# When the first token pair chooses its experts and when the first experts load, in a two-layer hybrid block

## The chip, the cores and the metric

The kernel runs on one core of one Trainium2 chip. The metric is the device time of one execution in microseconds (us); lower is better. Several executions are timed and their median is quoted; one further execution is recorded by the hardware profiler, and all rows below come from that one.

## The reference

Two layers act on 512 tokens of width 1024, in float32. Each layer mixes the tokens in three ways (block-sparse attention, a gated delta rule, a convolution), joins the three results to 1024 columns and multiplies them by `w_out`, the output projection. Then a hierarchical mixture of experts follows: each token picks one of 4 groups and the best 2 of the group's 8 experts.

```python
mix = jnp.concatenate([y_nsa, y_gdn, y_conf], axis=-1) @ w_out[l]
x = _layer_norm(DEEPNORM_ALPHA * x + mix, ln1_w[l], ln1_b[l])
moe = _hier_moe(x, ...)      # softmax over 4 groups, top 1; top 2 of 8 experts; gated FFN of width 512
x = _layer_norm(DEEPNORM_ALPHA * x + moe, ln2_w[l], ln2_b[l])
```

## The kernel before, in words

The tokens lie in four tiles of 128. The output projection (lines 1109 to 1162) works on them in two **pairs**, `pr` 0 and 1. For each pair it goes through `w_out` in four slices of 256 rows (`i`, 1 MB each), and each slice holds two blocks of 128 rows. So a pair has eight blocks. For a block, ScalarE casts the weights to a rounded high part (`wo_hi`, line 1135), VectorE or GpSimd subtracts that from the weights to get the rest (`wo_lo`, line 1136; GpSimd for rows `k` 1, 4 and 7), and TensorE does twelve matmuls (`mm3`, lines 355 to 357: three per token tile and half of the columns, into `opA` and `opB`). A matmul that reads `wo_lo` is line 356.

Three buffers bound how far ahead the weights can be prepared. The slices lie in a ring of three 1 MB tiles (`ring`, line 160), so a slice is loaded only when the third slice before it has been cast and subtracted. The tiles `wo_hi` and `wo_lo` share a ring of six (`WL`), so a block is cast only when TensorE is done with the third block before it. And the load instruction itself waits in SyncE's queue, which is in order.

After a pair's matmuls, lines 1142 to 1161 add the residual, transpose the two tiles, multiply them by the router's weights (`r_ps`, line 1155), normalize, and store the normalized tiles to `x1D` in HBM through SyncE's queue (line 1158). They leave the router's logits of the pair in `lg`. Then `top_k` (lines 1081 to 1107) chooses the experts of these two tiles: some 30 small VectorE instructions on 128 by 2 to 128 by 128 elements, with two exponentials on ScalarE in between (lines 1096 and 1098). It writes the selection `selb` and the weights `sw`. Both are used only after the second pair, from line 1203 on, where the tokens are counted per expert and ranked.

`load_expert` (lines 1180 to 1195) loads one expert: four tiles of gate and up weights (line 1187, two DMAs of 512 KB each) and two of down weights (line 1192, 1 MB each), six tiles of 1 MB. Two experts have fixed numbers (`N_STATIC`) and are loaded at line 1197; the other loads need numbers that are computed from the choice. Their tiles rotate through `ring` (3, the tiles that `w_out` used), `ring2` (9, free since the attention ended) and `ring3` (1). So of the twelve tiles of the first two experts three need the last three slices of `w_out` to be done, and nine do not. The buffers into which tokens are gathered are cleared on GpSimd (line 1201); they take the place of two tiles that hold parts of the mixed tokens, so a clear waits for the last matmul that reads those.

The order of each engine's instructions is not written by hand here. A scheduler goes through the program, with a forecast of its own for every duration, and gives each engine the instruction that is ready first by that forecast, and among ready ones the one that stands earlier in the program. Every engine and every DMA queue then runs its list in order. Only from the first expert on is TensorE's order that of the program (line 1511).

```python
for pr in range(2):                            # lines 1111 to 1162, shortened
    for i in range(4):
        nc.sync.dma_start(w, w_out[l, ...])    # 1126
        for kk in range(2):
            A.copy(hi[:, :1024], src)          # 1135
            (G if k in (1, 4, 7) else V).tensor_tensor(lo[:, :1024], src, hi, op=ALU.subtract)
            mm3(...)                           # 1139
    lg = osm("r_lg", [P, 2, 36])
    ...
    top_k(lg, 2 * pr)                          # 1162
weights = {30 + e: load_expert(e) for e in range(N_STATIC)}    # 1197
```

Of the kernel before, what the change touches and what calls it, by code (L numbers as in the profile page):

```python
# [29 lines left out]
N_STATIC = 2  # L30
# [82 lines left out]
def hybrid_kernel(ctx, tc, x_in, w_in, w_out, cmp_pe, cmp_w1, cmp_w2, conv_w, a_log, dt_bias, norm_w,  # L113
                  dw_w, dw_b, cln_w, cln_b, ln1_w, ln1_b, ln2_w, ln2_b, w_grp, b_grp, w_exp, b_exp,
                  w_gate, w_up, w_down, consts, out, R=3, R2=9, R4=1, NG=10, NE=9, WL=6, layers=DEPTH, CN=32, GI=2, CV0=5, CV1=30, CVM="A", EB=12, SC="GAGA", LB2="GGVVVVVV", TO="0123", HL=3, LOP=4, LOM="10110101", XP=6, ORDER="GkGcomGqPwfx0yG1t2z3GGr"):
    nc = tc.nc
# [25 lines left out]
    def tp(key, tag, bufs, name=None, dt=F32, n=1024):  # L142
        return pl[key].tile([P, n], dt, tag=tag, name=name or tag, bufs=bufs)
# [7 lines left out]
    def x4(name):  # L151
        return xp.tile([P, 1056], F32, tag="x4", name=name)
# [7 lines left out]
    def wring(name):  # L160
        return ring.tile([P, 2048], F32, tag="w", name=name)
# [10 lines left out]
    def bank2(name):  # L172
        return pl["psA"].tile([P, 2, 512], F32, tag="a", name=name)
# [16 lines left out]
    def C(name):  # L190
        o, n = _OFF[name]
        return cst[:, o - P:o - P + n] if o < _RES else cst2[:, o - _RES - S:o - _RES - S + n]
# [32 lines left out]
    def bc(ap, n):  # L225
        return ap.unsqueeze(len(ap.shape)).to_broadcast(list(ap.shape) + [n])
# [78 lines left out]
    for l in range(layers):  # L305
# [5 lines left out]
        for kp in range(4):  # L311
            a = tp("inp", "xT", 8, f"xTh{kp}", F32R)
            b = tp("inp", "xT", 8, f"xTl{kp}", F32R)
            for kk in range(2):
                k = 2 * kp + kk
# [494 lines left out]
        for step in ORDER:  # L810
# [175 lines left out]
            elif step in '0123':  # L986
# [14 lines left out]
                for g in range(2):  # L1001
# [3 lines left out]
                    for b in range(2):  # L1005
# [6 lines left out]
                        for i0 in range(0, 4, hb):  # L1012
                            ps = bankS("a_s")
                            for i in range(hb):
                                o = i * P if t == 0 else i * 256
                                w = min(Lc, 512 - o)
# [8 lines left out]
                            for i in range(hb):  # L1025
                                e = tp("att", "e", EB, n=512)
# [39 lines left out]
        def osm(name, shape, dt=F32, bufs=2):  # L1066
            return pl["osm"].tile(shape, dt, tag=name, name=name, bufs=bufs)
# [5 lines left out]
        def first_max(src, rev, mx, oh, scr):  # L1073
            V.tensor_reduce(mx, src, axis=AX.X, op=ALU.max)
            for t in range(2):
                V.scalar_tensor_tensor(scr[:, t, :], src[:, t, :], mx[:, t:t + 1], rev, op0=ALU.is_equal, op1=ALU.mult)
            mv = osm("r_mv", [P, 2])
            V.tensor_reduce(mv, scr, axis=AX.X, op=ALU.max)
            V.tensor_tensor(oh, scr, bc(mv, src.shape[2]), op=ALU.is_equal)

        def top_k(lg, t0):
            zg, ze = lg[:, :, 0:4], lg[:, :, 4:36]
            s4, ohg = osm("r_s4", [P, 2, 4]), osm("r_ohg", [P, 2, 4])
            mg, gw, m1, m2 = [osm(n, [P, 2]) for n in ("r_mg", "r_gw", "r_m1", "r_m2")]
            em, s32, oh1, oh2 = [osm(n, [P, 2, 32]) for n in ("r_em", "r_s32", "r_oh1", "r_oh2")]
            first_max(zg, C("rev4"), mg, ohg, s4)
            V.tensor_scalar(ohg, ohg, 1.0, -NEG, op0=ALU.subtract, op1=ALU.mult)
            V.tensor_tensor(em.rearrange("p t (g e) -> p t g e", e=8), ze.rearrange("p t (g e) -> p t g e", e=8), bc(ohg, 8),
                            op=ALU.add)
            first_max(em, C("rev32"), m1, oh1, s32)  # L1090
            V.scalar_tensor_tensor(em, oh1, 2.0 * NEG, em, op0=ALU.mult, op1=ALU.add)
            first_max(em, C("rev32"), m2, oh2, s32)
            V.tensor_tensor(selb[:, t0:t0 + 2], oh1.unsqueeze(2).to_broadcast([P, 2, 2, 32]),
                            oh2.unsqueeze(2).to_broadcast([P, 2, 2, 32]), op=ALU.add)
            V.tensor_tensor(s4, zg, bc(mg, 4), op=ALU.subtract)
            A.activation(s4, s4, AF.Exp)
            V.tensor_tensor(m2, m2, m1, op=ALU.subtract)
            A.activation(m2, m2, AF.Exp)
            V.tensor_reduce(gw, s4, axis=AX.X, op=ALU.add)
            V.reciprocal(gw, gw)  # L1100
            V.tensor_scalar(m1, m2, 1.0, None, op0=ALU.add)
            V.reciprocal(m1, m1)
            V.tensor_tensor(m1, m1, gw, op=ALU.mult)
            V.tensor_tensor(m2, m2, m1, op=ALU.mult)
            V.tensor_tensor(oh1, oh1, bc(m1, 32), op=ALU.mult)
            V.tensor_tensor(oh2, oh2, bc(m2, 32), op=ALU.mult)
            V.tensor_tensor(sw[:, t0:t0 + 2, 1, :], oh1, oh2, op=ALU.add)
# [3 lines left out]
        for pr in range(2):  # L1111
            for t in (2 * pr, 2 * pr + 1):
                xt = x4(f"xr{t}")
                A.dma_start(xt[:, :D], xsrc[t * P:(t + 1) * P, :])
                xr.append(xt)
            def lt(i, k, t):
                if k < 4:
                    return mp[t // 2][i][:, (t % 2) * 512 + k * P:(t % 2) * 512 + (k + 1) * P]
                return mp["GC"[(k - 4) // 2]][i][:, (k % 2) * 512 + t * P:(k % 2) * 512 + (t + 1) * P]

            ap = [bank2("opA"), bank2("opB")]
            for i in range(4):

                kq = (3, 0, 1, 2)[i]
                w = wring("w_out")
                nc.sync.dma_start(w.rearrange("p (k c) -> p k c", k=2),
                                  w_out[l, kq * 256:(kq + 1) * 256, :].rearrange("(k p) c -> p k c", p=P))
                if pr == 0 and i == 1:
                    for n, src in ((1, mxA[1]), ("G", mxG)):
                        mp[n] = mix_parts(src, tp("out", "mh", 2, dt=F32R)[:, :D], "mxA")  # L1130
                for kk in range(2):
                    k = 2 * kq + kk
                    src = w[:, kk * 1024:(kk + 1) * 1024]
                    hi, lo = tp("out", "whl", WL, "wo_hi", F32R), tp("out", "whl", WL, "wo_lo", F32R)
                    A.copy(hi[:, :1024], src)
                    (G if k in (1, 4, 7) else V).tensor_tensor(lo[:, :1024], src, hi[:, :1024].bitcast(F32), op=ALU.subtract)
                    for t in (2 * pr, 2 * pr + 1):
                        for n in range(2):
                            mm3(ap[t % 2][:, n, :], lt(0, k, t), lt(1, k, t), hi[:, n * 512:(n + 1) * 512],
                                lo[:, n * 512:(n + 1) * 512], i == 0 and kk == 0, i == 3 and kk == 1)  # L1140

            lg = osm("r_lg", [P, 2, 36])
            for t in (2 * pr, 2 * pr + 1):
                V.scalar_tensor_tensor(xr[t][:, :D], xr[t][:, :D], ALPHA, ap[t % 2].rearrange("p a b -> p (a b)"),
                                       op0=ALU.mult, op1=ALU.add)
            for t in (2 * pr, 2 * pr + 1):
                xT = tp("osm", "x1T", 2)
                for kq in range(2):
                    ps = bank("x1T_ps")
                    for kk in range(4):  # L1150
                        T.transpose(ps[:, kk * P:(kk + 1) * P], xr[t][:, 4 * kq + kk:1024:8], ident)
                    A.copy(xT[:, kq * 512:(kq + 1) * 512], ps)
                ps = bank("r_ps")
                for k in range(8):
                    T.matmul(ps[:, 0:36], xT[:, k * P:(k + 1) * P], wrw[:, k, :], start=(k == 0), stop=(k == 7))
                mu, rs, nb = norm_stats([xr[t][:, h * 512:(h + 1) * 512] for h in range(2)])
                A.activation(xr[t][:, :D], xr[t][:, :D], AF.Identity, scale=rs, bias=nb)
                nc.sync.dma_start(x1D[l][t * P:(t + 1) * P, :], xr[t][:, :D])
                d = osm("r_d", [P, 36])
                V.scalar_tensor_tensor(d, cs, mu, ps[:, 0:36], op0=ALU.mult, op1=ALU.add)  # L1160
                V.scalar_tensor_tensor(lg[:, t % 2, :], d, rs, rb2, op0=ALU.mult, op1=ALU.add)
            top_k(lg, 2 * pr)
        outR.close()
        outL.close()
        mixer.close()
# [14 lines left out]
        def load_expert(e):  # L1180

            wgu, wd = [], []
            s_ = slice(e, e + 1) if isinstance(e, int) else bass.ds(e, 1)
            for i in range(4):
                w = ering("w_gu")
                for wi, src in enumerate((w_gate, w_up)):
                    nc.sync.dma_start(w[:, wi * 1024:(wi + 1) * 1024].rearrange("p (k f) -> p k f", f=512),
                                      src[l, s_].rearrange("e (p k) f -> p (e k) f", k=8)[:, 2 * i:2 * i + 2, :])
                wgu.append(w)
            for i in range(2):  # L1190
                w = ering("w_d")
                nc.sync.dma_start(w.rearrange("p (k c) -> p k c", c=1024),
                                  w_down[l, s_, i * 256:(i + 1) * 256, :].rearrange("e (k p) c -> p (e k) c", p=P))
                wd.append(w)
            return wgu, wd

        weights = {30 + e: load_expert(e) for e in range(N_STATIC)}

        XG = [x4(f"xg{i}") for i in range(2)]
        for xg in XG:  # L1200
# [444 lines left out]
```

## Time and profile before

| | us |
|---|---|
| Median of three timed runs | 1949.95 |
| Lowest and highest of them | 1946.44, 1950.87 |
| The profiled execution, its own time | 1944.57 |
| Its span, first to last instruction | 1942.8 |

The profiled execution's time is its span and 1.77 us around it, and it is 5.38 us under the median of the timed runs. The mean granted clock of TensorE over the span is 0.931 of full speed. The page gives busy times per engine over the span; the timeline gives each engine's instructions with their start, their length, and in brackets how long the engine sat idle before them and what released it. Matmuls overlap in the pipeline, so the distance from one start to the next, not the length, is what a matmul costs.

### The profile page before, as it was taken

What the parts mean: (1) busy time and instruction counts of PE and PEld (TensorE: products, weight loads), DVE (VectorE), ACT (ScalarE), POOL (GpSimd) and SP (SyncE); (2) the same over time, 40 slices, a digit from 0 to 9 for tenths busy, and PEclk for the clock granted to TensorE, in tenths of its full rate; (3) what the DMA queues carried; (4) which work ended last, traced back from release to release, by engine and by line L of the source; (5) the groups of instructions that cost most, each with busy time, mean ns of one, the idle gap of its engine ahead of it and who ended that gap; (6) DMA issues with size and microseconds to landing.
All of it is one profiled execution on the core that took longest, in us unless ns stands there. A gap on an engine that the chain in (4) does not pass through costs nothing. (4 is left out here: it accounts for less than half of the span.)

```text
span 1942.8 us, 31345 instructions
## 1 busy us (share of the span) xinstructions
PE 1730.3 (89%) x11812; PEld 1016.1 (52%) x11812; DVE 1012.3 (52%) x2258; ACT 573.3 (30%) x1250; POOL 389.9 (20%) x354
## 2 busy tenths in 40 slices
PE   8898799969989899999789987998798898999996
PEld 6776576753443434333377765766634434343333
DVE  2756877454433524343637668765644325244435
ACT  3342565422211112111233325653322101121122
POOL 2234641413000000000222346423140000000001
PEclk9997599979999899999999976999899998999998
DMA  5221000758999989999632210008489999899994
GB/s 181 88 87 66 1 2 23 285 176 321 408 401 405 403 317 386 409 370 409 246 113 78 93 48 1 13 34 302 139 338 408 402 404 404 301 403 408 379 409 191
DMA packets 147339, 478.41 MB, mean 246 GB/s; under 512 B 23032, under 2 KB 25584, under 8 KB 147184
## 3 DMA queue, kind: packets, MB, share of 16 engines
q1 hardware_dynamic: 138304, 456.74, 61.4%
q10 hardware_dynamic: 4144, 10.70, 1.5%
q0 software_dynamic: 4736, 8.92, 1.3%
q8 instruction: 95, 1.56, 0.3%
q14 instruction: 60, 0.49, 0.1%
HBM read 476.04 MB, written 8.39 MB: 249 GB/s over the span
## 5 line engine op out<-in xcount | busy, mean ns | idle before, releaser
L1285 PE MATMUL f_gu<-w_gu,m_xe 128*32 128x256 f32 (+1 forms) x3456 | 400.4, 455 | 21.1 <-DMA w_gu<-in_moe_w_up 18.0
L1285 PEld LDWEIGHTS f_gu<-w_gu,m_xe 128*32 128x32 f32 (+1 forms) x3456 | 135.2, 118 | 273.2 <-issue 224.0
L1317 PE MATMUL f_y<-w_d,f_hTs 128*32 128x256 f32 (+2 forms) x1824 | 252.5, 474 | 9.2 <-ACT f_hTs L1302 2.9
L1327 DVE TENSOR_TENSOR m_yl<-f_y,m_yh 32x256 fp32r<-32x256 f32 (+2 forms) x222 | 115.2, 520 | 257.5 <-ACT m_yh L1325 249.8
L1325 ACT CAST m_yh<-f_y 32x256 fp32r<-32x256 f32 (+2 forms) x222 | 98.6, 444 | 299.0 <-PE f_y L1317 296.7
L1377 POOL DMA_INDIRECT xg<-x1D,m_idx x34 | 36.0, 1059 | 748.4 <-PE f_hT L1300 331.7
L1438 DVE TENSOR_TENSOR xr<-xr,m_sc 128x1024 f32<-128x1024 f32 x128 | 153.1, 1219 | 25.9 <-PE m_sc L1437 24.6
L1317 PEld LDWEIGHTS f_y<-w_d,f_hTs 128*32 128x32 f32 (+2 forms) x1824 | 82.6, 124 | 156.9 <-issue 126.7
L1292 DVE SCALAR_TENSOR_TENSOR f_h<-f_h,m_wsl,f_gu 128x128 f32<-128x128 f32 (+1 forms) x76 | 33.0, 434 | 227.8 <-ACT f_h L1291 227.4
L1291 ACT ACTIVATE f_h<-f_gu 128x128 f32<-128x128 f32 (+1 forms) x76 | 26.5, 348 | 388.5 <-PE f_gu L1285 289.4
L1437 PE MATMUL m_sc<-m_yh,m_ohT 128*128 128x512 f32 (+1 forms) x256 | 115.0, 449 | 28.8 <-DVE xr L1438 28.5
L351 POOL TENSOR_TENSOR w_hl<-w_slice,w_hl 128x512 fp32r<-128x512 f32 (+1 forms) x54 | 70.4, 1306 | 250.8 <-ACT w_hl L350 241.8
L1437 PE MATMUL m_sc<-m_yl,m_ohT 128*128 128x512 f32 (+1 forms) x256 | 104.0, 406 | 0.0
L350 ACT CAST w_hl<-w_slice 128x512 fp32r<-128x512 f32 (+1 forms) x96 | 56.2, 590 | 144.1 <-PE ipB L357 115.5
L1281 PE MATMUL f_gu<-w_gu,m_xe 128*128 128x512 f32 x192 | 88.7, 607 | 0.4 <-DMA w_gu<-in_moe_w_gate 0.3
L1437 PEld LDWEIGHTS m_sc<-m_yh,m_ohT 128*128 128x128 f32 (+1 forms) x256 | 49.7, 194 | 65.9 <-DVE xr L1438 43.7
L766 POOL TENSOR_TENSOR cvt<-cvt,cv_t 128x485 f32<-128x485 f32 (+28 forms) x66 | 77.7, 1179 | 14.6 <-ACT cv_t L762 12.7
L1028 ACT ACTIVATE e<-a_s,a_nm 128x128 f32<-128x128 f32 (+3 forms) x128 | 66.6, 528 | 42.0 <-DVE a_nm L1023 37.7
L1420 PE MATMUL m_g<-ident,xg 128*128 128x128 f32 (+2 forms) x272 | 48.0, 300 | 19.9 <-DMA xg<-x1D,m_idx 16.6
L1281 PEld LDWEIGHTS f_gu<-w_gu,m_xe 128*128 128x128 f32 x192 | 35.2, 192 | 52.8 <-issue 48.8
L351 DVE TENSOR_TENSOR w_hl<-w_slice,w_hl 128x512 fp32r<-128x512 f32 (+1 forms) x42 | 30.1, 717 | 62.4 <-ACT w_hl L350 62.1
L1363 ACT ACTIVATE m_xe<-m_g,b1c,w1c 128x256 f32<-128x256 f32 (+3 forms) x72 | 37.2, 541 | 79.7 <-DVE m_xe L1365 79.5
(474 smaller groups left out, 3335.7 us busy)
## 6 DMA issues: line engine op xcount, KB each, us to landing
w_gu<-in_moe_w_gate SPq DMA_DIRECT2D x256, 512.0 KB
w_gu<-in_moe_w_up SPq DMA_DIRECT2D x256, 512.0 KB
w_d<-in_moe_w_down SPq DMA_DIRECT2D x128, 1024.0 KB
w_slice<-in_w_in SPq DMA_DIRECT2D x20, 1024.0 KB
w_out<-in_w_out SPq DMA_DIRECT2D x16, 1024.0 KB
x1D<-xr SPq DMA_DIRECT2D x8, 512.0 KB
w_slice<-in_w_in SPq DMA_DIRECT2D x4, 560.0 KB
x<-in_x SPq DMA_DIRECT2D x4, 512.0 KB
```

The lines of the kernel that those rows point to most:

```text
L350: A.copy(hi[:, :n], src)
L351: (G if LOE(npc[0], k) else V).tensor_tensor(lo[:, :n], src, hi[:, :n].bitcast(F32), op=ALU.subtract)
L766: G.tensor_tensor(ac2[:, 30 - j:512], ac2[:, 30 - j:512], tm, op=ALU.add)
L1028: A.activation(e[:, :L], ps[:, i * L:(i + 1) * L], AF.Exp, bias=nm[:, i:i + 1], accum_out=sums[:, i0 + i:i0 + i + 1])
L1281: T.matmul(pg[:, i, :], xe(k), wv[:, i, :], start=(k == 0), stop=(k == 7), skip_group_check=True)
L1285: T.matmul(pg[j * c:(j + 1) * c, 0, 0:2 * fw], xe(k), wv[:, :, j * fw:(j + 1) * fw], start=(k == 0), stop=(k == 7), skip_group_check=True)
L1317: T.matmul(o, lt, wv[:, n * nw:(n + 1) * nw], start=(k == 0), stop=(k == 3), skip_group_check=True)
L1325: A.copy(hi[:, n * nw:(n + 1) * nw], src[n])
L1327: V.tensor_tensor(lo[:, n * nw:(n + 1) * nw], src[n], hi[:, n * nw:(n + 1) * nw].bitcast(F32), op=ALU.subtract)
L1420: T.transpose(ps[:, kk * 256 + u * P:kk * 256 + u * P + m], XG[u][0:m, k:1024:8], ident[0:m, 0:m])
L1437: T.matmul(ps2[:, n, :], ohT[0:nr, t * P:(t + 1) * P], y[0:nr, n * 512:(n + 1) * 512], start=(i == 0), stop=(i == 1))
L1438: V.tensor_tensor(xr[t][:, :D], xr[t][:, :D], ps2.rearrange("p a b -> p (a b)"), op=ALU.add)
```

## The change

`top_k` of the first pair moves from the end of the first pair to behind the loop over the second pair's slices (it still reads the first pair's `lg`, since the new `lg` is made below it). And the DMAs of the first two experts get an edge that puts each of them behind the load of the last slice of `w_out` in SyncE's queue: `issue_after` orders the issue and waits for no transfer. No instruction is added or removed.

```diff
--- before.py
+++ after.py
@@ -1123,7 +1123,7 @@
 
                 kq = (3, 0, 1, 2)[i]
                 w = wring("w_out")
-                nc.sync.dma_start(w.rearrange("p (k c) -> p k c", k=2),
+                w_last = nc.sync.dma_start(w.rearrange("p (k c) -> p k c", k=2),
                                   w_out[l, kq * 256:(kq + 1) * 256, :].rearrange("(k p) c -> p k c", p=P))
                 if pr == 0 and i == 1:
                     for n, src in ((1, mxA[1]), ("G", mxG)):
@@ -1138,6 +1138,9 @@
                         for n in range(2):
                             mm3(ap[t % 2][:, n, :], lt(0, k, t), lt(1, k, t), hi[:, n * 512:(n + 1) * 512],
                                 lo[:, n * 512:(n + 1) * 512], i == 0 and kk == 0, i == 3 and kk == 1)
+            if pr:
+
+                top_k(lg, 0)
 
             lg = osm("r_lg", [P, 2, 36])
             for t in (2 * pr, 2 * pr + 1):
@@ -1159,7 +1162,8 @@
                 d = osm("r_d", [P, 36])
                 V.scalar_tensor_tensor(d, cs, mu, ps[:, 0:36], op0=ALU.mult, op1=ALU.add)
                 V.scalar_tensor_tensor(lg[:, t % 2, :], d, rs, rb2, op0=ALU.mult, op1=ALU.add)
-            top_k(lg, 2 * pr)
+            if pr:
+                top_k(lg, 2)
         outR.close()
         outL.close()
         mixer.close()
@@ -1194,7 +1198,9 @@
                 wd.append(w)
             return wgu, wd
 
-        weights = {30 + e: load_expert(e) for e in range(N_STATIC)}
+
+        with tc.issue_after(w_last.ins):
+            weights = {30 + e: load_expert(e) for e in range(N_STATIC)}
 
         XG = [x4(f"xg{i}") for i in range(2)]
         for xg in XG:
```

## Rows read from the trace of the kernel before

**Rows 1.** The page, part 1: busy time of TensorE over the whole span.

```profile
PE 1730.3 (89%) x11812; PEld 1016.1 (52%) x11812; DVE 1012.3 (52%) x2258; ACT 573.3 (30%) x1250; POOL 389.9 (20%) x354
```

**Rows 2.** TensorE's instructions, layer 0: start us, length us, line, operation [idle before, releaser].

```profile
381.21 0.48 PE L355 MATMUL opA<-wo_hi,mh 128*128 128x512 f32 x1
...
396.48 0.39 PE L357 MATMUL opB<-wo_hi,ml 128*128 128x512 f32 x1
...
400.25 0.80 PE L355 MATMUL opA<-wo_hi,mh 128*128 128x512 f32 x1 [3.38 <-ACT wo_hi L1135]
...
406.77 0.39 PE L355 MATMUL opB<-wo_hi,mh 128*128 128x512 f32 x1
...
414.50 0.39 PE L357 MATMUL opB<-wo_hi,ml 128*128 128x512 f32 x1
```

**Rows 3.** Stretches of 5 us, layer 0: busy time (instructions) per engine, granted clock, DMA.

```profile
375.00:380.00 5.00, 5.00 (x23) 3.90 (x21) 2.21 (x2) 1.56 (x2) 2.06 (x2) 1.00 1.02 408
...
385.00:390.00 5.00, 5.00 (x36) 4.58 (x35) 3.12 (x4) 3.83 (x5) 3.04 (x3) 1.00 0.95 214
...
400.00:405.00 5.00, 4.30 (x9) 2.98 (x10) 2.94 (x7) 2.09 (x3) 2.84 (x1) 0.50 0.47 160
```

**Rows 4.** ScalarE's instructions, layer 0, around TensorE's stall.

```profile
396.36 0.21 ACT L1096 ACTIVATE r_s<-r_s 128x8 f32<-128x8 f32 x1 [5.88 <-DVE r_s L1095]
399.05 0.20 ACT L1098 ACTIVATE r_m<-r_m 128x2 f32<-128x2 f32 x1 [2.48 <-DVE r_m L1097]
399.16 2.92 ACT L1135 CAST wo_hi<-w_out 128x1024 fp32r<-128x1024 f32 x3
```

**Rows 5.** VectorE's instructions, layer 0: first and last of the first pair's choice.

```profile
395.10 0.16 DVE L1074 TENSOR_REDUCE r_mg<-r_lg 128x2 f32<-128x8 f32 x1
...
400.51 0.23 DVE L1107 TENSOR_TENSOR r_sw<-r_oh,r_oh 128x64 f32<-128x64 f32 x1
```

**Rows 6.** SyncE's queue of DMA issues, layer 0.

```profile
357.05 0.45 SPq L1187 DMA_DIRECT2D w_gu<-in_moe_w_gate  x1
...
385.98 3.46 SPq L1126 DMA_DIRECT2D w_out<-in_w_out  x2
...
421.02 1.46 SPq L1158 DMA_DIRECT2D x1D<-xr  x2
```

**Rows 7.** TensorE's instructions, layer 1: the stall, then the second pair's first and last.

```profile
1345.32 0.40 PE L355 MATMUL opB<-wo_hi,mh 128*128 128x512 f32 x1
1348.39 0.50 PE L356 MATMUL opA<-wo_lo,mh 128*128 128x512 f32 x1 [2.68 <-POOL wo_lo L1136]
...
1352.37 0.39 PE L355 MATMUL opA<-wo_hi,mh 128*128 128x512 f32 x1
...
1356.13 0.47 PE L355 MATMUL opA<-wo_hi,mh 128*128 128x512 f32 x1
...
1382.30 0.39 PE L357 MATMUL opB<-wo_hi,ml 128*128 128x512 f32 x1
```

**Rows 8.** ScalarE's casts of the seventh and the ninth block, layer 1.

```profile
1339.50 1.05 ACT L1135 CAST wo_hi<-w_out 128x1024 fp32r<-128x1024 f32 x1 [1.78 <-PE opB L356]
...
1345.98 1.04 ACT L1135 CAST wo_hi<-w_out 128x1024 fp32r<-128x1024 f32 x1 [2.67 <-DMA w_out<-in_w_out]
```

**Rows 9.** GpSimd's instructions, layer 1, at the same stall.

```profile
1345.08 0.95 POOL L1201 MEMSET xg<- 128x1024 f32 x1 [10.31 <-PE opB L356]
1345.99 2.34 POOL L1136 TENSOR_TENSOR wo_lo<-w_out,wo_hi 128x1024 fp32r<-128x1024 f32 x1
```

**Rows 10.** SyncE's queue, layer 1: the last four slices of w_out.

```profile
1334.79 21.48 SPq L1126 DMA_DIRECT2D w_out<-in_w_out  x4
```

**Rows 11.** GpSimd, layer 0: the first gather of tokens.

```profile
434.62 1.11 POOL L1377 DMA_INDIRECT xg<-x1D,m_idx  x1 [13.89 <-DVE m_idx L1374]
```

**Rows 12.** TensorE: first matmuls with an expert's weights, layer 0, then layer 1.

```profile
439.98 1.98 PE L1285 MATMUL f_gu<-w_gu,m_xe 128*64 128x512 f32 x4
...
1407.37 1.98 PE L1285 MATMUL f_gu<-w_gu,m_xe 128*64 128x512 f32 x4
```

## The prediction

> **What bounds the kernel now.** I began with the page: TensorE is busy for 89% of the span [rows 1], so an edit that takes no work off TensorE can only gain where TensorE stands still or runs at the lower clock. Then I read TensorE's timeline through the output projection of both layers, for gaps. There is one in each layer, and each has another cause.
>
> In layer 0 it lies in the second pair. The matmul of 396.48 is followed by one at 400.25, released by a cast on ScalarE; in the stretch behind it the granted clock is 0.50, that is 1.2 GHz instead of 2.4, and only at 406.77 do the matmuls follow each other at the old distance [rows 2, 3]. The 35 matmuls from 406.77 to 414.50 are 0.227 us apart (7.73 over 34 steps). So the gap costs 400.25 - 396.48 - 0.23 = 3.54 us. The 13 matmuls that start from 400.25 up to 406.77 take 6.52 us where 13 x 0.227 = 2.96 would do: 3.56 us more. Together 7.10 us.
>
> Why was the cast late? ScalarE sat idle for 5.88 us before the first exponential of `top_k` and for 2.48 us before the second, each time waiting for VectorE, and the casts start 0.11 us after the second [rows 4]. The whole choice on VectorE runs from 395.10 to 400.74, 30 instructions [rows 5]. So the next cast stood in ScalarE's queue behind the first pair's choice. The reader should also see when its weights were asked for: the first experts' DMAs begin at 357.05, and the last two slices of `w_out` are issued only at 385.98, behind nine of the twelve expert tiles [rows 6]. A late landing in the scheduler's forecast is a reason to put the choice ahead of the casts.
>
> In layer 1 the gap lies in the first pair: from 1345.32 to 1348.39, released by a `wo_lo` of GpSimd [rows 7]. It costs 1348.39 - 1345.32 - 0.23 = 2.84 us, and the ten matmuls from 1348.39 to 1352.37 take 3.98 us instead of 2.27: 1.71 more. Together 4.55 us. The choice has no part in it. The block's cast was done at 1340.55 [rows 8], but GpSimd's queue had the clear of a gather buffer first; that waited 10.31 us for the matmuls that free the buffer, and the `wo_lo` ran from 1345.99 to 1348.33 [rows 9]. Such an order is sensible only if the forecast had the slice land late. The trace has such a lateness: the slices issued from 1334.79 on [rows 10] let ScalarE wait for a DMA until 1345.98 [rows 8].
>
> **The change, part by part.** *The choice moved.* Its 30 VectorE instructions, its two exponentials and their waits stay; no DMA and nothing of SyncE or GpSimd is in it. Behind the second pair's loop in the program, the pair's casts outrank it on ScalarE. What hides it is the rest of the second pair: the logits are ready at 395.1, the choice takes 5.64 us [rows 5], and the pair's matmuls last until 414.5, or 407.4 without the stall [rows 2]. So I cost it at 0; without that cover it would cost 5.64 us a layer, because the counting behind the pair needs both pairs' `selb`. The gain is the 7.10 us of layer 0, provided the weights are there, which the second part sees to. A check from elsewhere: layer 1's second pair has no gap and runs from 1356.13 to 1382.30, 26.17 us [rows 7]; layer 0's runs from 381.21 to 414.50, 33.29 us [rows 2]. The difference is 7.12.
>
> *The experts moved.* In each layer 16 DMAs of 0.5 MB and 4 of 1 MB are moved past all slices of `w_out` in SyncE's queue. `w_out` then has the DMA engines for itself, and a slice's issue waits for its ring buffer alone. In layer 1 the clear should then fall behind the `wo_lo`, as the forecast has the slice early: 4.55 us. I take all of it; the other end is 0, if the clear stays ahead for another reason.
>
> What the move costs is cover for the experts. Twelve tiles of 1.05 MB are 12.58 MB; at 408 GB/s [rows 3] that is 30.8 us. In layer 0 the last slice's issue ends at 389.44 at the latest [rows 6], so all experts have landed by 420.3. They are first read at 439.98 [rows 12], or 432.9 with the gain: 12.6 us are left. In layer 1 the last slice is issued at 1356.27 [rows 10], less 4.55; the experts land by 1382.5, and are read at 1407.37 - 4.55 = 1402.8 [rows 12]. So 0. In the same queue behind them are the stores of `x1D`, whose second half is issued at 421.02 in layer 0 [rows 6] (413.9 then), with the DMA engines busy until 420.3. Both pairs' stores are 2.1 MB, 5.1 us at 408 GB/s: landed by 425.4, while the first gather starts at 434.62 - 7.10 = 427.5 [rows 11]. Two us are left, so 0 again, and every us over that would be paid in full. The loads of the next layer's router weights pass on the same queue and are needed a layer later.
>
> **Sum.** 7.10 + 4.55 = 11.65 us. From the profiled execution's 1944.57 that gives 1932.9. The median of the timed runs lies 5.38 above that execution, so on its scale the forecast is 1949.95 - 11.65 = 1938.3 us.
>
> **The rivals.** *One layer only* gains: 1942.9 with layer 0's part, 1945.4 with layer 1's. For it speaks that the two stalls have different causes and different cures, and that the orders come from a forecast that I can't see.
>
> *The choice goes into the tail.* If the first pair's choice lands behind the second pair's residual on VectorE, it lies on the chain that everything waits for: 2 x 5.64 = 11.28 us given back, 1949.6 us, no change. Against it speaks that VectorE has idle time while the second pair's matmuls run (2.94 of 5 us busy [rows 3]) and that the choice outranks the residual in the program.
>
> *GpSimd's clears get ahead (slower).* Each layer has two clears, in one queue with `wo_lo`. If the new order puts one ahead of a `wo_lo` that TensorE needs first, it costs what layer 1 shows, 4.55 us. If layer 1 keeps its one and three more appear (layer 1's second, both of layer 0), then layer 0 gives -7.10 + 9.10 and layer 1 +4.55: 6.55 us slower, 1956.5. It decides from two clears ahead in layer 0 on, which already eat its gain. Against it: earlier slices make the `wo_lo` ready earlier and the clears no sooner; in layer 0 no clear is in the way now.
>
> *The experts land late (slower).* The lowest rate while DMA was busy is 214 GB/s, in one stretch of 5 us [rows 3]. If it held throughout, 12.58 MB would take 58.8 us, to 448.2 in layer 0 and 1410.5 in layer 1: 15.3 and 7.7 us too late, 23.0 - 11.65 = 11.4 us slower, 1961.3. The rate around it was twice that. The Trainium skill, "DMA: Bandwidth & Descriptors", section "Rules for kernel authors", says to issue a DMA early and to wait for it late, and the change does the opposite for 12 MB. By that rule this rival would come true as soon as the slack is gone; the rows show 12.6 us of slack at the full rate.
>
> **How the numbers follow.** Both gains 0.50; one layer only 0.16; the choice in the tail, or another stall that gives back as much, 0.18; the clears 0.12; the experts late 0.04. A measurement of this kernel can tell some 0.2% (3.9 us) from no change. The first two cases are faster by more (0.66), the third is the same (0.18), the last two are slower (0.16). The range goes from 1932, the sum counted from the lower, profiled time, to 1950, no change; above it lie the slower cases. The likeliest case's own range is 1932 to 1942.
>
> **What would show each step.** In the changed profile, layer 0's second pair should last some 26 us at a granted clock of 1.00 throughout, with the casts ahead of the exponentials on ScalarE and the choice done before the pair's last matmul. In layer 1 the clear should stand behind the `wo_lo` and the first pair should have no gap near its seventh block. SyncE should show all slices of `w_out` ahead of the first expert. TensorE's first expert matmul should still wait for the gathered tokens, not for weights, and come 7 and then 11.7 us earlier. I am wrong if a gap of some 3 us with the lower clock behind it stands at another block, if a `top_k` instruction follows the second pair's residual, or if the gather starts later after the second `selb` than before.

## The result, and the profile after

The changed kernel takes 1940.34 us in the median of 20 runs; the kernel before, run beside it, 1949.43 us (20 runs). The medians lie 9.1 us apart. The ratio on record is 0.9942, with a 95% interval of 0.9926 to 0.9959, and that is what I go by: 11.3 us faster, between 8.0 and 14.4. The forecast was 11.65 us and 1938.3 us.

The profiled execution of the changed kernel has a span of 1940.6 us, only 2.2 under the one before (1942.8). A span can't carry this result: a second profiled execution of the very same changed kernel, further down, has 1932.4. So I compare stages, between markers that both kernels have: VectorE's residual of the first pair, that of the second pair, and the first matmul with an expert's weights. The last column runs from the last token tile's first attention matmul on compressed keys (`a_cmp`, 1277.29 us in the kernel before) to layer 1's first residual, and holds that layer's first pair; it is left out where TensorE runs that stretch in yet another order. Each number is the difference of two starts in the timelines; the ratios stand with the runs.

| kernel | layer 0: residual to residual | layer 1: the same | 2nd residual to first expert matmul, layers 0 and 1 | layer 1: `a_cmp` to 1st residual |
|---|---|---|---|---|
| before | 34.78 | 27.65 | 26.18, 25.77 | 76.66 |
| after | 27.63 | 27.64 | 26.26, 26.21 | 71.68 |
| choice moved only | 35.24 | 27.64 | 26.25, 25.88 | 76.69 |
| loads moved only | 27.63 | 27.64 | 26.17, 26.16 | 70.09 |
| clears moved only | 34.75 | 27.64 | 26.18, 25.84 | 72.08 |
| choice forced behind the casts | 35.18 | 27.64 | 26.29, 25.94 | 76.68 |
| choice forced behind casts and `wo_lo` | 27.63 | 27.64 | 26.28, 25.73 | 75.61 |
| after, choice forced ahead | 34.86 | 35.03 | 26.31, 26.27 | |
| after, choice in the tail | 27.63 | 27.64 | 30.02, 29.95 | 70.11 |
| after, loads behind the last store of `x1D` | 27.63 | 27.66 | 29.01, 28.99 | |
| both orders by hand, loads unmoved | 27.63 | 27.66 | 26.17, 25.91 | 72.07 |
| after, second execution | 27.63 | 27.66 | 26.23, 26.19 | 70.59 |

Layer 0's second pair is 7.15 us shorter. Of the changed kernel, SyncE's queue in layer 0 (start, length, line, operation), beside [rows 6]:

```profile
371.44 13.35 SPq L1126 DMA_DIRECT2D w_out<-in_w_out  x3
384.83 0.46 SPq L1191 DMA_DIRECT2D w_gu<-in_moe_w_gate  x1
...
417.50 1.46 SPq L1161 DMA_DIRECT2D x1D<-xr  x2
```

All of `w_out` is now ahead of the first expert, which is asked for at 384.83 instead of 357.05; the last stores of `x1D` come 3.5 us earlier than before. ScalarE of the changed kernel in the same stretch, beside [rows 4]:

```profile
395.80 1.05 ACT L1135 CAST wo_hi<-w_out 128x1024 fp32r<-128x1024 f32 x1 [0.77 <-PE opB L356]
400.33 1.05 ACT L1135 CAST wo_hi<-w_out 128x1024 fp32r<-128x1024 f32 x1 [3.48 <-PE opB L356]
401.29 0.20 ACT L1096 ACTIVATE r_s<-r_s 128x8 f32<-128x8 f32 x1
403.06 1.05 ACT L1135 CAST wo_hi<-w_out 128x1024 fp32r<-128x1024 f32 x1 [1.57 <-PE opB L356]
405.26 0.20 ACT L1098 ACTIVATE r_m<-r_m 128x2 f32<-128x2 f32 x1 [1.15 <-DVE r_m L1097]
```

Before, both exponentials stood ahead of the casts and each waited for VectorE. Now a cast waits for nothing but TensorE, that is for a free buffer, and the exponentials fall in between. VectorE still ends the choice in time, 2.4 us ahead of the second pair's residual (its timeline, beside [rows 5]):

```profile
407.85 0.23 DVE L1107 TENSOR_TENSOR r_sw<-r_oh,r_oh 128x64 f32<-128x64 f32 x1
410.26 1.22 DVE L1147 SCALAR_TENSOR_TENSOR xr<-xr,opA 128x1024 f32<-128x1024 f32 x1 [2.19 <-PE opA L357]
```

The stretches of 5 us of the changed kernel show TensorE without a gap and at the full granted clock, where [rows 3] had 0.50 at 400:

```profile
395.00:400.00 5.00, 5.00 (x32) 4.42 (x31) 4.11 (x12) 1.08 (x2) 0.00 (x0) 1.00 1.02 408
400.00:405.00 5.00, 5.00 (x24) 4.14 (x23) 4.36 (x13) 2.21 (x3) 2.39 (x1) 1.00 1.03 412
405.00:410.00 5.00, 5.00 (x24) 4.14 (x23) 2.90 (x12) 0.20 (x1) 0.00 (x0) 1.00 1.04 414
```

In layer 1, GpSimd's queue of the changed kernel, beside [rows 9]:

```profile
1335.96 2.40 POOL L1136 TENSOR_TENSOR wo_lo<-w_out,wo_hi 128x1024 fp32r<-128x1024 f32 x1 [12.68 <-ACT wo_hi L1135]
1340.41 0.95 POOL L1207 MEMSET xg<- 128x1024 f32 x1 [2.05 <-PE opB L356]
```

The clear stands behind the `wo_lo` of the seventh block, and behind its first matmul TensorE has no wait of over 0.6 us in that pair.

More has changed there than the clear. TensorE's own list is another one: the first matmuls with `wo_hi` now stand among the last attention matmuls (`a_o`), 41.39 us behind the marker of the last column where it was 48.13. Two shorter waits of the kernel before, in the same pair as the gap of [rows 7], are gone as well. TensorE of the kernel before, then of the changed one:

```profile
1326.80 0.50 PE L356 MATMUL opA<-wo_lo,mh 128*128 128x512 f32 x1 [0.64 <-DVE wo_lo L1136]
...
1331.48 0.50 PE L356 MATMUL opA<-wo_lo,mh 128*128 128x512 f32 x1 [1.63 <-POOL wo_lo L1136]
```

```profile
1314.65 0.50 PE L355 MATMUL opA<-wo_hi,mh 128*128 128x512 f32 x1 [0.80 <-ACT wo_hi L1135]
...
1315.31 0.65 PE L1050 MATMUL a_o<-a_pTs,kvb 128*64 128x256 f32 x4
```

So the length of this pair no longer compares, and the last column is the measure. The lists of all engines differ also outside these stretches. What that is worth there the profiles can't tell: from layer 0's first expert matmul to the marker, the kernels with the old order of TensorE took 834 to 841 us and those with the new one 836 to 838.

The experts start as before: TensorE waits for the gathered tokens, 6.32 us here and 6.27 before, and not for weights (its timeline, beside [rows 12]):

```profile
435.32 0.91 PE L1426 MATMUL m_g<-ident,xg 128*128 128x128 f32 x3 [6.32 <-DMA xg<-x1D,m_idx]
...
436.52 1.98 PE L1291 MATMUL f_gu<-w_gu,m_xe 128*64 128x512 f32 x4
...
1398.79 1.98 PE L1291 MATMUL f_gu<-w_gu,m_xe 128*64 128x512 f32 x4
```

### The profile page after: what moved, and what is told of

Read it like the earlier page. It is cut to its first block, busy times and chain, and to the rows that moved or that the text cites. A ratio compares the mean times of both kernels' runs of the same rounds, so it can differ in the third digit from the quotient of the medians.

```text
span 1940.6 us, 31342 instructions
## 1 busy us (share of the span) xinstructions
PE 1726.5 (89%) x11812; PEld 1013.2 (52%) x11812; DVE 1010.8 (52%) x2258; ACT 573.2 (30%) x1250; POOL 390.0 (20%) x354
## 5 line engine op out<-in xcount | busy, mean ns | idle before, releaser
L1023 DVE TENSOR_REDUCE a_nm<-a_s 128x1 f32<-128x384 f32 (+3 forms) x88 | 55.3, 635 | 11.9 <-PE a_s L1020 11.0
```

The source lines that it names most:

```text
L1023: V.tensor_reduce(nm[:, 0:hb], ps[:, :hb * L].rearrange("p (h l) -> p h l", h=hb), axis=AX.X, op=ALU.max, negate=True)
```

## The experiments

**One part at a time.** The first run has the choice moved as in the change and the loads where they were; the second the loads moved and the choice at its old place.

```diff
+            if pr:
+                top_k(lg, 0)
...
-            top_k(lg, 2 * pr)
+            if pr:
+                top_k(lg, 2)
```

> The choice is moved in the program as in the change; the experts' loads stay where they were before. Theory A (the loads make the whole gain; a choice written further down changes no engine's order, since the scheduler places instructions by its forecast of when their data are ready and not by their place in the text): the ratio to the kernel before is 1.000, layer 0's second pair still has the TensorE gap of about 3.5 us with the 1.2 GHz stretch behind it, and from the first pair's residual to the second's pass about 34.8 us, as before. Theory B (the prediction's step: behind the loop the casts outrank the choice): layer 0's gap is gone, residual to residual about 27.7 us, the ratio 0.9964 (7.1 us of 1950); layer 1's first-pair gap stays in both.

```diff
-        weights = {30 + e: load_expert(e) for e in range(N_STATIC)}
+        with tc.issue_after(w_last.ins):
+            weights = {30 + e: load_expert(e) for e in range(N_STATIC)}
```

> The experts' loads issue behind the last slice of w_out as in the change; the choice stays at its old place in the program. Theory A (loads alone): everything the change gained, ratio 0.994, layer 0 residual to residual 27.6 us with no gap, layer 1's first pair without the 2.8 us gap. Theory B (the prediction's split): only layer 1's 4.55 us, ratio 0.9977, with layer 0's second pair as before (34.8 us residual to residual).

Choice alone: ratio 0.9982 (0.9960 to 1.0004), no gain that can be told from none. ScalarE of that kernel shows the old order, with the waits of 5.88 and 2.48 of [rows 4] to the hundredth:

```profile
401.50 0.21 ACT L1096 ACTIVATE r_s<-r_s 128x8 f32<-128x8 f32 x1 [5.88 <-DVE r_s L1095]
404.19 0.20 ACT L1098 ACTIVATE r_m<-r_m 128x2 f32<-128x2 f32 x1 [2.48 <-DVE r_m L1097]
404.30 2.92 ACT L1135 CAST wo_hi<-w_out 128x1024 fp32r<-128x1024 f32 x3
```

In its trace every engine's instructions stand in the order of the kernel before; the text moved, the order didn't. Loads alone: ratio 0.9942 (0.9922 to 0.9962), and its instructions stand in the order of the changed kernel. Its stretches, with the clock at 1.00:

```profile
400.00:405.00 5.00, 5.00 (x24) 4.14 (x23) 4.36 (x13) 2.21 (x3) 2.39 (x1) 1.00 1.02 409
```

So theory A holds: the move of the loads makes the whole gain, and the move of `top_k` none of it, in either layer. That an edge on SyncE's DMAs reorders ScalarE, VectorE, GpSimd and TensorE must come through the scheduler's forecast, which takes the casts to be ready earlier when `w_out` is asked for early; this link follows from how the scheduler works and is not itself seen in a run. The next runs ask whether the order is the cause, or the earlier weights themselves.

**Layer 1's clears.** The kernel before, with only the clears moved.

```diff
+                    if k == 4:
+                        g_last = sub       # the wo_lo of row k on GpSimd
...
-        for xg in XG:
-            G.memset(xg[:, :D], 0.0)
+        with tc.issue_after(g_last.ins):
+            for xg in XG:
+                G.memset(xg[:, :D], 0.0)
```

> The kernel before, with only the two clears of the gather buffers put behind the last wo_lo of GpSimd. If the clear ahead of a wo_lo made layer 1's gap (prediction's reading of the first pair): the gap of 2.84 us at about 1345 and the slow stretch of 1.71 us behind it go, 4.5 us, ratio 0.9977, and layer 0 keeps its gap. If the late w_out slices made it, and the clear only stood in a wait that was there anyway: the gap stays, TensorE then waits at the same place for a cast or for GpSimd, ratio 1.000.

Ratio 0.9963 (0.9947 to 0.9980). Layer 1's first pair loses its gap: from its first matmul to its residual 23.96 us instead of 28.53, 4.57 less, where 2.84 + 1.71 = 4.55 was read from [rows 7]. Layer 0 keeps its own. GpSimd of this kernel in layer 1:

```profile
1343.14 2.41 POOL L1136 TENSOR_TENSOR wo_lo<-w_out,wo_hi 128x1024 fp32r<-128x1024 f32 x1 [5.86 <-ACT wo_hi L1135]
...
1373.07 1.85 POOL L1204 MEMSET xg<- 128x1024 f32 x2
```

No load was moved, and the `wo_lo` of the seventh block ran right behind its cast. The clear's place was the cause of this gap.

The 1.71 us in it are the slow clock behind the gap, and they are not paid in every execution. Behind the same wait of 2.68 us the clock fell in the kernel before (0.88 and 0.78 in the stretches from 1345 and 1350 us), and it fell in the run with the choice moved only and in the next run below. In the one after that it did not, and the pair took 26.97 us:

```profile
1345.00:1350.00 5.00, 5.00 (x24) 3.88 (x23) 1.89 (x3) 1.62 (x2) 2.12 (x1) 1.00 0.60 210
```

**Layer 0's order, on ScalarE alone.** The kernel before, with an edge that puts the choice behind the last cast.

```diff
+            if pr:
+                with tc.issue_after(cast.ins):
+                    top_k(lg, 0)
```

> The kernel before with its loads where they were, and the first pair's choice forced behind the second pair's last cast, so that ScalarE's exponentials really queue behind the casts. If the order of ScalarE's queue made layer 0's gap (the prediction's reading): the gap is gone, residual to residual about 27.7 us, 7 us gained in layer 0, although the weights are still asked for late. If the late landing of the last two w_out slices, which were asked for behind nine expert tiles, made it: the casts wait for a DMA in place of the exponentials, and a gap of 1 to 4 us stays at the same block.

Ratio 1.0009 (0.9993 to 1.0025), and the gap stayed, but as neither theory had it. The edge holds on the engine of the cast only, so VectorE's list is nearly the old one. Its rows, then ScalarE's and TensorE's:

```profile
393.75 0.16 DVE L1074 TENSOR_REDUCE r_mg<-r_lg 128x2 f32<-128x8 f32 x1
...
396.93 2.50 DVE L1076 SCALAR_TENSOR_TENSOR r_s<-r_em,r_m,cst 128x32 f32<-128x32 f32 x2
...
400.18 2.35 DVE L1136 TENSOR_TENSOR wo_lo<-w_out,wo_hi 128x1024 fp32r<-128x1024 f32 x2
```

```profile
392.24 2.00 ACT L1135 CAST wo_hi<-w_out 128x1024 fp32r<-128x1024 f32 x2 [3.12 <-DMA w_out<-in_w_out]
395.89 1.04 ACT L1135 CAST wo_hi<-w_out 128x1024 fp32r<-128x1024 f32 x1 [1.66 <-DMA w_out<-in_w_out]
```

```profile
401.45 0.80 PE L356 MATMUL opA<-wo_lo,mh 128*128 128x512 f32 x1 [5.49 <-DVE wo_lo L1136]
```

The casts now run when their slices land, and the wait moved to the next queue: `wo_lo` stands behind the choice on VectorE and starts 5.9 us after both casts were done (394.24). The late slices cost ScalarE 3.12 and 1.66 us of waiting, but TensorE worked without a gap until its matmul of 395.57.

**The same on both engines.** Still the loads of before; the choice behind the seventh block's cast on ScalarE and the sixth block's `wo_lo` on VectorE.

```diff
+            if pr:
+                with tc.issue_after(c4.ins), tc.issue_after(s3.ins):    # cast of k = 4, wo_lo of k = 3
+                    top_k(lg, 0)
```

> The kernel before, its loads where they were; the first pair's choice is forced behind the casts of the second pair's seventh block on ScalarE and behind the wo_lo of its sixth on VectorE, so that it queues behind the weights on both engines. If the order in those two queues made layer 0's gap: the casts run when their slices have landed (392.2 and 395.9 us in the run where ScalarE alone was reordered), the wo_lo right behind them, TensorE has no gap over 1 us in the second pair, residual to residual is 27.6 to 28.5 us instead of 34.8, with the weights still asked for as late as before; ratio about 0.9965, layer 1 keeping its gap. If the late landing of the slices made it: TensorE stands still at the same block for 1 to 4 us, residual to residual 30 us or more.

Ratio 0.9960 (0.9935 to 0.9984), residual to residual 27.63 us, as in the changed kernel. ScalarE of this kernel, then its stretches:

```profile
395.72 2.00 ACT L1135 CAST wo_hi<-w_out 128x1024 fp32r<-128x1024 f32 x2 [3.85 <-DMA w_out<-in_w_out]
399.12 1.05 ACT L1135 CAST wo_hi<-w_out 128x1024 fp32r<-128x1024 f32 x1 [1.40 <-DMA w_out<-in_w_out]
400.33 0.21 ACT L1096 ACTIVATE r_s<-r_s 128x8 f32<-128x8 f32 x1 [0.15 <-DVE r_s L1095]
```

```profile
395.00:400.00 5.00, 5.00 (x27) 4.27 (x27) 3.60 (x9) 2.88 (x3) 0.00 (x0) 1.00 0.98 340
400.00:405.00 5.00, 5.00 (x24) 4.15 (x23) 4.83 (x14) 1.44 (x3) 2.39 (x1) 1.00 1.03 416
```

The slices are as late as before and the casts wait for them, yet TensorE has no gap: at that point it works on blocks prepared ahead. The late landing cost nothing by itself; the order did. TensorE's own list is that of the kernel before in this run, so its new order in the changed kernel isn't needed for layer 0's gain.

**The counter-test.** The changed kernel, its loads behind `w_out`, with the old order forced: choice ahead of the second pair's last four casts and of its `wo_lo` on VectorE there.

```diff
+                if pr and i == 2:
+                    ex, swi = top_k(lg, 0)       # its second exponential, its last VectorE instruction
...
+                    with (tc.issue_after(ex.ins) if pr and i >= 2 else ExitStack()):
                         A.copy(hi[:, :1024], src)
```

(and the same with `swi` for the subtraction on VectorE)

> The kernel after, its loads behind w_out; the first pair's choice is forced ahead of the second pair's last four casts on ScalarE and of its last two wo_lo on VectorE, the order that stood in layer 0 before. If the order in the queues is what cost the time, the early slices are no help: layer 0's gap of about 3.5 us and the slow stretch come back, residual to residual about 34 us, and layer 1, where the choice never stood ahead of the casts, gets the same gap for the first time; 13 us slower than the changed kernel, ratio to the kernel before about 1.001. If early landing is what brought the time: residual to residual stays near 28 us in both layers, ratio 0.994.

Ratio 1.0006 (0.9980 to 1.0033): the gain is given back. Layer 0 has its gap again (34.86 us), and layer 1 gets one that it never had (35.03 instead of 27.64). TensorE and ScalarE of this kernel in layer 1:

```profile
1375.57 0.50 PE L355 MATMUL opA<-wo_hi,mh 128*128 128x512 f32 x1 [3.38 <-ACT wo_hi L1138]
```

```profile
1371.68 0.21 ACT L1096 ACTIVATE r_s<-r_s 128x8 f32<-128x8 f32 x1 [5.88 <-DVE r_s L1095]
1374.38 0.20 ACT L1098 ACTIVATE r_m<-r_m 128x2 f32<-128x2 f32 x1 [2.48 <-DVE r_m L1097]
1374.49 2.92 ACT L1138 CAST wo_hi<-w_out 128x1024 fp32r<-128x1024 f32 x3
```

The three casts waited for no DMA, only for their turn. The Trainium skill, "PSUM — Partial Sum Buffer", section "Engine vs sequencer instructions", says that the queues of ScalarE, VectorE and GpSimd are strictly first in, first out; this trace agrees, with 5.88 + 2.48 us in which ScalarE was idle.

**Both orders by hand.** The edit on both engines and that of the clears together on the kernel before (choice behind, clears behind), no load moved; and the changed kernel again, beside the same runs of the kernel before.

> The kernel before with its experts' loads where they were, ahead of the last slices of w_out, and with both orders put right by hand: the first pair's choice behind the second pair's casts and wo_lo, and the two clears behind GpSimd's last wo_lo. If the change gained through the order of three engines' queues and through nothing else, this gains as much without moving a load: residual to residual 27.6 us in layer 0, no gap in layer 1's first pair, ratio 0.993 to 0.996. If the loads' place matters by itself too (DMA engines free for w_out, the stores of x1D behind the loads): 0.997 or more, with waits of the casts or of the gather longer than in the changed kernel.

> The changed kernel itself, on the same chip and beside the same runs of the kernel before as the run with both orders put right by hand, so that the two ratios can be compared: 0.994, as first measured.

By hand 0.9942 (0.9918 to 0.9965), the changed kernel 0.9934 (0.9904 to 0.9964): the same gain without the move, as far as the ratios can tell. In the kernel by hand the casts still wait for the DMA:

```profile
404.26 2.00 ACT L1135 CAST wo_hi<-w_out 128x1024 fp32r<-128x1024 f32 x2 [3.25 <-DMA w_out<-in_w_out]
407.63 1.05 ACT L1135 CAST wo_hi<-w_out 128x1024 fp32r<-128x1024 f32 x1 [1.37 <-DMA w_out<-in_w_out]
```

In layer 0 freeing the DMA engines for `w_out` is worth nothing: 27.63 us either way. In layer 1 the last column leaves something: 72.07 us by hand against 70.1 to 70.6 in the three other profiles with the changed kernel's list there (71.68 in its first, where the clock fell). The kernel by hand has TensorE's list of before and keeps the waits of 0.64 and 1.65 us. Whether these 1.5 to 2.0 us come from the new list or from weights that were asked for earlier, no run separates.

**The choice in the tail.** The changed kernel, with the first pair's choice behind the second pair's last logits, to price that rival.

```diff
+                with tc.issue_after(rlg.ins):    # the last r_lg, line 1164
+                    top_k(lg0, 0)
```

> The kernel after, with the first pair's choice forced behind the last logits of the second pair, on the chain that everything waits for. The prediction's price for that rival is the choice's full 5.64 us in each layer: second residual to the first expert matmul 31.9 us instead of 26.2, in both layers, 11.3 us in all, ratio to the kernel before about 1.000. If the two choices overlap on VectorE (two chains of short instructions that wait on themselves), it costs less: 2 to 4 us in each layer, ratio 0.996 to 0.998.

Ratio 0.9971 (0.9947 to 0.9995). From the second residual to the first expert matmul it is 30.02 - 26.26 = 3.76 us longer in layer 0 and 29.95 - 26.21 = 3.74 in layer 1: 7.5 us, not 11.28. TensorE, where the counting waits:

```profile
421.78 0.21 PE L1213 MATMUL r_pos<-r_selb,trib 128*128 128x32 bf16 x1 [5.13 <-DVE r_selb L1093]
...
425.44 0.19 PE L1213 MATMUL r_pos<-r_selb,trib 128*128 128x32 bf16 x1 [3.34 <-DVE r_selb L1093]
```

Counting needs `selb` only; the second one comes 3.66 us after the first, since the choices overlap and their weights `sw` come later.

**Later still.** The changed kernel, with the experts behind the last store of `x1D`.

```diff
-                nc.sync.dma_start(x1D[l][t * P:(t + 1) * P, :], xr[t][:, :D])
+                w_last = nc.sync.dma_start(x1D[l][t * P:(t + 1) * P, :], xr[t][:, :D])
```

> The kernel after, with the experts' loads put later still: behind the last store of x1D, so from about 418 us in layer 0, some 33 us later than in the changed kernel. If the experts need their cover whole (the prediction's way of counting the rival that they land late): 12.58 MB at 408 GB/s land by 449 us, the first expert matmul waits for weights until then instead of 436.5, 12 us in each layer, ratio to the kernel before about 1.006. If the tiles are wanted one after the other as the experts go, the first is there in time: the first expert matmul starts within 2 us of where it did, the waits for w_gu behind it grow by less than 5 us, ratio 0.994 to 0.998. The gather of the tokens shares the DMA engines with them and may come later by a few us in either case.

Ratio 1.0167 (1.0130 to 1.0205): 44 us slower than the changed kernel, worse than either theory. SyncE, TensorE and ScalarE of this kernel in layer 0:

```profile
414.46 0.39 SPq L1191 DMA_DIRECT2D w_gu<-in_moe_w_gate  x1
```

```profile
433.45 1.12 PE L1426 MATMUL m_g<-ident,xg 128*128 128x128 f32 x4 [9.09 <-DMA xg<-x1D,m_idx]
...
470.86 0.69 PE L1306 MATMUL f_hT<-ident,f_h 128*128 128x128 f32 x2 [10.59 <-DVE f_h L1298]
```

```profile
468.29 0.34 ACTq L244 DMA_DIRECT2D ln_w<-in_ln_w  x1
469.53 0.34 ACTq L244 DMA_DIRECT2D ln_b<-in_ln_b  x1
469.91 0.38 ACT L1297 ACTIVATE f_h<-f_gu 128x256 f32<-128x256 f32 x1 [16.84 <-DMA w_gu<-in_moe_w_up]
```

The tiles came in time for the first expert; it started 2.75 us later (29.01 instead of 26.26), for the gather, which shared the DMA engines with them: they moved 407 GB/s from 428 to 433 us, while it was under way, against 231 from 430 to 435 in the changed kernel. The second wait of TensorE comes through a queue, and late weights are at its head: ScalarE issued two DMAs at 468.29 and 469.53 (453.83 and 454.22 in the changed kernel), the activation stands behind them, and its row names a load of `w_gu` as what ended ScalarE's 16.84 us of waiting. TensorE stood 10.59 us for that activation. The like in layer 1 is 9.4 us. That names 2 x 2.75 + 10.59 + 9.4 = 25.5 of the 44; TensorE's list also differs from the changed kernel's in the first part of layer 1, and the rest I did not take apart. The Trainium skill, "DMA: Bandwidth & Descriptors", section "Rules for kernel authors", says to issue early and wait late. The direction agrees here; but moved back by 24 us, as the change did (from 22.0 us ahead of layer 0's first residual to 2.2 behind it), the loads delayed no expert in layer 0, and moved back by 34 more (36.5 behind it) they cost 44. The measurement decides how far "early" goes.

## Why the prediction was right, and which step was wrong

The forecast of 11.65 us lies in the measured interval, 8.0 to 14.4. Layer 0's term was of the right size: 7.10 read from the gap and the slow stretch, 7.15 measured (34.78 - 27.63). Layer 1's was right for the gap that it was read from, 4.55 against 4.57 with the clears moved alone, and too small for the change: 6.07 in the second execution of the changed kernel (76.66 - 70.59), and 4.98 in the first, where the clock fell and that pair took 1.6 us longer than in the second. "There is one in each layer" passed over the waits of 0.64 and 1.63 us.

The number is partly luck. Both parts are in the change, so a gain credited to the wrong part could not show in the total.

- **The bottleneck.** Right: two stalls of TensorE and the slow clock behind them, one from ScalarE's queue, one from GpSimd's.
- **"The choice moved. … Behind the second pair's loop in the program, the pair's casts outrank it on ScalarE."** This step failed. The choice moved alone changed no engine's order and no time (0.9982, 0.9960 to 1.0004). Place in the program decides only among instructions that the forecast holds ready, and there the casts, with their weights asked for late, were not: so I read it, the forecast itself is not among the traces. So "the gain is the 7.10 us of layer 0, provided the weights are there" credited the wrong part: the proviso did the work, and through the order alone, since the same order by hand gains as much in layer 0 with late weights.
- **"The experts moved … the clear should then fall behind the `wo_lo`, as the forecast has the slice early."** Right, and its reason, the slice early in the forecast, would serve for layer 0's casts too.
- **Costs of 0.** Right but for 0.4 us: the wait for the gather is 6.32 us (6.27 before), and the first expert matmul doesn't wait for weights; in layer 1 it comes 26.21 us behind the second residual instead of 25.77.
- **What would show each step.** The second pair lasts 27.6 us from residual to residual at a clock of 1.00, and the choice is done 2.4 us ahead of the residual, as forecast. The exponentials stand among the casts, not behind all of them. The first expert matmul came 3.5 and 8.6 us earlier, not 7 and 11.7: this execution was 3.6 us later already at layer 0's first residual (382.63 against 379.02), which the second one was not (378.44; its expert matmuls came 7.7 and 12.6 earlier).
- **One layer only.** The reason given for it, "different causes and different cures", was half right: two causes, as the single-order runs show, and one cure.
- **The tail.** Its price was too high: 3.75 us a layer, since only the way to `selb` counts, not the whole choice of 5.64.
- **The clears get ahead.** They did not: layer 1's stands behind the `wo_lo`, and behind layer 0's two TensorE has no wait in the second pair.
- **The experts land late.** Not at this distance. Placed 34 us further back it is real, and dearer than the slack that I counted: the first expert's tiles were in time, and what held TensorE was the gather and ScalarE's queue behind a load of weights.

No kernel run here beats the changed one by more than its interval.

## What to carry to other kernels

Where a scheduler orders the queues by forecast readiness, moving a block in the text may do nothing, while an edge on a DMA can reorder every compute engine, far from the place that was meant: compare the engines' orders before crediting a part. When two things change at once, test the queue order and the data's arrival apart, by forcing the order with the loads unmoved and the old order with the loads moved. And where a short chain waits on itself in a queue ahead of long independent work, force it behind on every engine it uses: on one alone, the wait moves to the next queue.

## What the runs showed of the hardware that was not expected

The granted clock fell without a gap. In both layers of the changed kernel's first profiled execution, some 3.5 us of the matmuls behind those of `r_const` (26 of 128x36 in layer 0, the last of them done at 366.9 us) ran at the lower level, 1.2 GHz, though TensorE had no wait in the 10 us before; in the second execution of the same kernel they ran at 2.4 GHz. The stretch at 365 us, first execution, then the second (which is 2.7 us ahead here, and at 1.00 in the stretch at 360 too):

```profile
365.00:370.00 5.00, 5.00 (x25) 4.35 (x25) 2.64 (x4) 2.51 (x3) 0.00 (x0) 0.68 0.13 4
```

```profile
365.00:370.00 5.00, 5.00 (x23) 4.00 (x23) 1.91 (x2) 2.10 (x2) 0.53 (x1) 1.00 0.38 55
```

From layer 0's first pair's first matmul to its residual the one took 32.61 us and the other 31.07: 1.5 us. What decides it these runs don't show.

A small VectorE instruction can take ten times its length. In the changed kernel, `r_oh` (128x64) took 2.34 us beside a `wo_lo` on GpSimd, and 0.22 later without one. VectorE, then GpSimd:

```profile
401.60 2.34 DVE L1079 TENSOR_TENSOR r_oh<-r_s,r_mv 128x64 f32<-128x64 f32 x1
...
405.19 0.22 DVE L1079 TENSOR_TENSOR r_oh<-r_s,r_mv 128x64 f32<-128x64 f32 x1
```

```profile
401.46 2.39 POOL L1136 TENSOR_TENSOR wo_lo<-w_out,wo_hi 128x1024 fp32r<-128x1024 f32 x1 [7.24 <-ACT wo_hi L1135]
```

The Trainium skill, "SBUF — State Buffer", section "Who interferes with whom", says that a VectorE instruction with two SBUF inputs contends with a GpSimd instruction that reads SBUF, through a port pair that is an exclusive lock. The trace agrees: the `wo_lo` began 0.14 us earlier, and `r_oh` ended 0.09 us after it. In the run with ScalarE alone reordered the same cost about 2.1 us inside the choice (2.50 us for the pair at 396.93, 0.41 elsewhere): by this arithmetic the whole of the difference between its gap, 5.49 us, and the 3.38 of [rows 2].
